# Even and odd last columns on two paths, target loaded further forward, and the rest column of target issued from ScalarE

## The chip, the cores and the metric

One core of one Trainium2 chip runs the kernel; the other seven are idle. The metric is device time in microseconds (us), the median of several executions. The profile's span (first to last instruction) is some 1.7 us shorter than that time. Executions of the kernel before agree within 0.05 us in six runs. All runs with rounds (repeated beside the kernel before) that are compared below are in the fast state, that is, none is over 1.5% above the fastest of its kernel; the one single look is marked.

## The reference

```python
# pred, target: (32, 147, 768) f32
mean = target.mean(-1, keepdims=True)
var = target.var(-1, keepdims=True)
target = (target - mean) / np.sqrt(var + 1e-6)
loss = np.mean((pred - target) ** 2, axis=-1)
return loss.mean(axis=-1)                      # (32,)
```

Both inputs are read once: 2 x 32 x 147 x 768 x 4 bytes = 28.9 MB. The output is 32 numbers.

## The kernel before

The 4704 rows lie on 128 partitions as 36 full "columns" of 128 rows and one "rest" column of 96 rows; a column is 128 x 768. VectorE takes mean and variance of each target column (two statistics, one aggregation), ScalarE and VectorE make `1/sqrt(var)`, GpSimd normalises into `s` (bf16). A *unit* is one or two columns, and its squared difference goes one of three ways:

- **"ACT"**: TensorE forms `pred - s` in PSUM (the memory that its products go to) with two identity products, ScalarE squares and sums it.
- **"DVE+ACT"**: VectorE subtracts in SBUF (the working memory), ScalarE squares and sums.
- **"DVE"**: VectorE subtracts, squares and sums.

Small matmuls with a mask add everything up at the end.

```python
# order of loads; "hw" = Sync's queue, f32; the others GpSimd's queue, f32 read, bf16 written
piece("t", 0, 4, q="hw"); piece("t", REST, REST + 1, q="hw")
# ... t4, p_rest, t8, p0, t12, t16, p4, t20, p8 ...
piece("t", 24, 28); piece("p", 12, 16)
piece("t", 28, 32); piece("p", 16, 20)
piece("t", 32, 36)
# ... pred 20 to 31 in twos, 32, 33, 34 alone, 35 in halves

groups = [tuple(range(0, 4)), (REST,)] + [tuple(range(c, c + 4)) for c in range(4, KM, 4)]
units = [((c, c + 1), 0, D, "ACT" if c < 22 else "DVE+ACT") for c in range(0, KM - 4, 2)]
# ... 28 "DVE", 29 "DVE+ACT", (30, 31) "DVE+ACT", 32 "DVE", 33 "DVE+ACT", 34 "DVE",
#     35 as two halves "ACT"

def normalise(u, c):                     # GpSimd
    # ...
    pin(nc.gpsimd.tensor_scalar(out=s[:n, so:so + D], in0=til[:n, o:o + D], scalar1=nm, scalar2=r,
                                op0=ALU.add, op1=ALU.mult))

def difference(u, d0, w):                # VectorE, two inputs in SBUF
    # ...
    pin(nc.vector.tensor_tensor(out=z[:, :w], in0=til[:, o:o + w], in1=s[:, so + d0:so + d0 + w],
                                op=ALU.subtract))

psum = ctx.enter_context(tc.tile_pool(name="psum", bufs=2, space=bass.MemoryType.PSUM))   # z: 3 banks each
```

Every operation is listed with an estimated duration, and a greedy list schedule in the kernel's own Python fixes each engine's program order. The engines then run in that order.

Of the kernel before, what the change touches and what calls it, by code (L numbers as in the profile page):

```python
# [7 lines left out]
F32 = mybir.dt.float32  # L8
BF16 = mybir.dt.bfloat16
ALU = mybir.AluOpType  # L10
ACTF = mybir.ActivationFunctionType
# [3 lines left out]
def kernel(  # L15
# [7 lines left out]
    nc = tc.nc  # L23
    pin = tc.keep_in_program_order
    B, N, D = pred.shape
    eps = 1e-6
    P = 128
    J = P // B
    KJ = (N + J - 1) // J
    KM = N - (J - 1) * KJ  # L30
    assert KJ == KM + 1
    RP = B * (J - 1)
    half = D // 2
    BANK = 512
    REST = KM
# [4 lines left out]
    def rows_of(c):  # L40
        return RP if c == REST else P

    data = ctx.enter_context(tc.tile_pool(name="data", bufs=1))
# [3 lines left out]
    singles = ctx.enter_context(tc.tile_pool(name="singles", bufs=1))  # L47
# [5 lines left out]
    stream = []  # L53

    def piece(kind, c0, c1, d0=0, d1=D, q="sw"):
        stream.append((kind, c0, c1, d0, d1, q))

    piece("t", 0, 4, q="hw")
    piece("t", REST, REST + 1, q="hw")
    piece("t", 4, 8)  # L60
    piece("p", REST, REST + 1)
    piece("t", 8, 12)
# [2 lines left out]
    piece("t", 16, 20)  # L65
    piece("p", 4, 8)
    piece("t", 20, 24)
    piece("p", 8, 12)
    piece("t", 24, 28)
    piece("p", 12, 16)  # L70
    piece("t", 28, 32)
    piece("p", 16, 20)
    piece("t", 32, 36)
    for c in range(20, 24, 2):
        piece("p", c, c + 2)
    for c in range(24, 32, 2):
        piece("p", c, c + 2)
    for c in range(32, 35):
        piece("p", c, c + 1)
# [1 line left out]
    piece("p", KM - 1, KM, half, D)  # L81


    groups = [tuple(range(0, 4)), (REST,)] + [tuple(range(c, c + 4)) for c in range(4, KM, 4)]


    units = [((c, c + 1), 0, D, "ACT" if c < 22 else "DVE+ACT") for c in range(0, KM - 4, 2)]
    units.insert(2, ((REST,), 0, D, "ACT"))
    units += [((KM - 4,), 0, D, "DVE"), ((KM - 3,), 0, D, "DVE+ACT"), ((KM - 2,), 0, D, "DVE"),
              ((KM - 1,), 0, half, "ACT"), ((KM - 1,), half, D, "ACT")]  # L90
    k = units.index(((KM - 8, KM - 7), 0, D, "DVE+ACT"))
    units[k:k + 1] = [((KM - 8,), 0, D, "DVE"), ((KM - 7,), 0, D, "DVE+ACT")]



# [3 lines left out]
    def op(name, engine, dur, needs, fn, rank=0.0, early=0.0):  # L99
        by_name[name] = len(ops)  # L100
        ops.append((name, engine, dur, needs, fn, rank, early))
# [4 lines left out]
    def load(kind, c0, c1, d0, d1, q):  # L106
        x = targ_f if kind == "t" else pred_f
        n, w = rows_of(c0), d1 - d0
        til = data.tile([P, (c1 - c0) * w], F32 if q == "hw" else BF16, name=f"{kind}{c0}_{d0}")
        src = bass.AP(tensor=x.tensor, offset=x.offset + c0 * D + d0,  # L110
                      ap=[[N * D, B], [KJ * D, J - 1 if c0 == REST else J], [1, (c1 - c0) * w]])
        eng = nc.sync if q == "hw" else nc.gpsimd
        pin(eng.dma_start(out=til[:n], in_=src))  # L113
        for c in range(c0, c1):
            KIND[kind].setdefault(c, []).append((d0, d1, til, (c - c0) * w))


    land, lanes, clock, last = {}, {"hw": [], "sw": []}, 2.9, {}
    for i, (kind, c0, c1, d0, d1, q) in enumerate(stream):
        w = (c1 - c0) * (d1 - d0)  # L120
        clock += w * rows_of(c0) / P * 0.915 / D + (0.0 if w >= 4 * D else 0.04)
        lanes[q].append(clock + 1.1)
        for c in range(c0, c1):
            land[kind, c, d0] = clock + 1.1
        k = len(lanes[q])
        op(("load", i), "SP" if q == "hw" else "POOL", 0.6, [], lambda a=stream[i]: load(*a), rank=-1.0,
           early=0.0 if k <= 8 else lanes[q][k - 9] + 0.3)

    def landed(kind, c):
# [124 lines left out]
        pin(nc.vector.scalar_tensor_tensor(out=z, in0=z, scalar=1.0, in1=z, op0=ALU.mult, op1=ALU.mult,  # L254
                                           accum_out=dest))

    tail = 4
    n_early = len(units) - 1 - tail
    rl = singles.tile([P, n_early], F32)
    rl_sum = singles.tile([P, 1], F32)  # L260
    finals = []
    early_ops, users, seen = [], [], set()
    for k, (u, d0, d1, eng) in enumerate(units):
        w = len(u) * D if len(u) > 1 else d1 - d0
# [32 lines left out]
        users.append(("sq", k))  # L297

    acc = psum1.tile([1, B], F32)
    op("rl_sum", "DVE", 0.2, early_ops, lambda: pin(nc.vector.tensor_reduce(  # L300
        out=rl_sum, in_=rl, axis=mybir.AxisListType.X, op=ALU.add)), rank=50.0)
    finals.insert(0, ("rl_sum", rl_sum, mask, P))
    turn = []

# [7 lines left out]

    HOP = 0.15
    free = {e: 0.0 for e in ("SP", "POOL", "DVE", "ACT", "PE")}
    free["ACT"] = 2.1
    end, left, order = {}, list(range(len(ops))), []
    while left:
        best = None
        for i in left:
            name, engine, dur, needs, fn, rank, early = ops[i]  # L320
            if any(x not in end for x in needs):
                continue
            t = max([free[engine], early] + [end[x] + (0.0 if ops[by_name[x]][1] == engine else HOP) for x in needs])
# [4 lines left out]
        _, i, t = best  # L328
        name, engine, dur, needs, fn, rank, early = ops[i]
# [43 lines left out]
```

## Time and profile before

| | before |
|---|---|
| time, us | 77.8 |
| span, us | 76.0 |
| HBM read over the span | 28.90 MB, 380 GB/s |
| VectorE, GpSimd, ScalarE busy | 69%, 71%, 41% |
| DMA traffic ends | about 71.0 |
| last normalisation on GpSimd ends | 69.2 |
| copy of the result starts | 73.85 |

The lines that carry the reading stand in the prediction below. Lines from the timeline of the end: start, duration, engine, what, count, in brackets the idle time before it and what ended it.

```profile
66.22 1.41 DVE L249 TENSOR_TENSOR zd<-p,s 128x768 bf16<-128x768 bf16 x2 [1.11 <-DMA p<-in_pred_dram]
68.44 2.50 DVE L249 TENSOR_TENSOR zd<-p,s 128x1536 bf16<-128x1536 bf16 x3
```

Two single columns in 1.41 us, then a pair and two singles in 2.50. The fastest single difference in this trace takes 0.54. GpSimd is normalising beside them until 69.2. The views merge neighbouring instructions; their single records in the trace show that only two of these differences are slow: column 28 takes 0.95 us, and the pair 30 and 31 takes 1.56, where a pair takes 0.92 to 0.96 elsewhere.

### The profile page before, as it was taken

The numbers are of one execution on the slowest core, as the hardware profiler recorded it, in microseconds if no ns is written. First come the engines' busy times: TensorE is split into PE (matmuls) and PEld (weight loads), VectorE is DVE, ScalarE is ACT, GpSimd is POOL, SyncE is SP. The second block draws the span as 40 slices with busy tenths as digits, with TensorE's granted clock in tenths as the row PEclk, the third lists the DMA queues.
The fourth block names the chain that finished last, engine by engine and source line by source line (L and its number), as shares of the span: only waits on it lengthen the run. The fifth ranks groups of instructions, "written<-read, shape, count | busy, mean of one in ns | idle before, by whom it ended". The sixth has DMA issues, their size and how long they took to land.

```text
span 76.0 us, 535 instructions
## 1 busy us (share of the span) xinstructions
PE 29.5 (39%) x85; PEld 8.8 (12%) x86; DVE 52.3 (69%) x139; ACT 31.1 (41%) x61; POOL 54.0 (71%) x76
## 2 busy tenths in 40 slices
PE   0000000056898940679187708751642200004550
PEld 0000000011323300212031103110111000001020
DVE  0000499999999999927960896099429995499960
ACT  5100000400269501088019503940591669952960
POOL 4998205299998987598986898984488839994000
PEclk9999999999999999999965995699999555555555
DMA  0899999999999999999999999999999999999400
GB/s 0 213 420 310 251 228 236 210 220 213 210 217 217 213 214 217 217 210 213 217 217 217 213 215 217 210 220 210 220 199 212 210 215 210 216 200 201 61 0 0
DMA packets 3830, 15.41 MB, mean 203 GB/s; under 512 B 435, under 2 KB 1171, under 8 KB 3699
## 3 DMA queue, kind: packets, MB, share of 16 engines
q0 software_dynamic: 3568, 13.52, 88.2%
q1 hardware_dynamic: 258, 1.87, 6.8%
q14 instruction: 4, 0.02, 0.1%
HBM read 28.90 MB, written 0.00 MB: 380 GB/s over the span
## 4 chain that ended last, share of the span: by engine, by line
DMA 66%; DVE 21%; POOL 7%; issue 2%; PE 1%; ACT 0%; POOLq 0%; DVEq 0%; ACTq 0%
DMA t<-in_target_dram 49%; DMA p<-in_pred_dram 17%; DVE st L163 13%; POOL s L213 6%; DVE mv L164 3%; DVE zd L254 3%; DVE zd L249 2%; POOL p L113 1%; PE acc L307 1%; ACT r L187 0%; DVE r L193 0%; DVE ob L336 0%; POOLq L213 0%; DVEq L249 0%; ACTq L187 0%
## 5 line engine op out<-in xcount | busy, mean ns | idle before, releaser
L163 DVE BATCH_NORM_STATS2 st<-t 128x6 f32<-128x384 bf16 (+2 forms) x74 | 36.1, 530 | 14.2 <-DMA t<-in_target_dram 14.2
L213 POOL TENSOR_SCALAR s<-t,nm,r 128x768 bf16<-128x768 bf16 (+2 forms) x37 | 38.2, 1038 | 4.3 <-DVE r L193 2.2
L227 PE MATMUL z<-s,nident 128*128 128x512 bf16 (+3 forms) x36 | 13.8, 499 | 31.3 <-POOL s L213 26.9
L242 ACT ACTIVATE z<-z 128x1536 f32<-128x1536 f32 (+2 forms) x13 | 17.0, 1311 | 12.0 <-PE z L227 12.0
L227 PE MATMUL z<-p,ident 128*128 128x512 bf16 (+3 forms) x35 | 14.2, 548 | 12.2 <-DMA p<-in_pred_dram 12.0
L113 POOL DMA_DIRECT2D p<-in_pred_dram x17 | 9.6, 566 | 9.2 <-DMA t<-in_target_dram 4.3
L187 ACT ACTIVATE r<-mv,eps_t 128x4 f32<-128x4 f32 (+1 forms) x10 | 2.9, 293 | 26.8 <-DVE mv L164 26.1
L249 DVE TENSOR_TENSOR zd<-p,s 128x768 bf16<-128x768 bf16 (+1 forms) x9 | 7.3, 842 | 2.1 <-DMA p<-in_pred_dram 1.1
L242 ACT ACTIVATE zd<-zd 128x1536 bf16<-128x1536 bf16 (+1 forms) x6 | 7.6, 1264 | 2.8 <-DVE zd L249 2.8
L164 DVE BATCH_NORM_AGGREGATE mv<-st 128x2 f32<-128x12 f32 (+1 forms) x37 | 7.7, 209 | 1.3
L227 PEld LDWEIGHTS <-nident 128*128 128x128 bf16 (+1 forms) x37 | 3.4, 113 | 42.3 <-issue 23.0
L227 PEld LDWEIGHTS <-ident 128*128 128x128 bf16 (+1 forms) x37 | 4.8, 129 | 19.8 <-issue 18.5
L113 POOL DMA_DIRECT2D t<-in_target_dram x8 | 4.8, 622 | 1.0 <-POOLq L354 0.8
L193 DVE RECIPROCAL r<-r 128x4 f32<-128x4 f32 (+1 forms) x10 | 1.5, 148 | 2.8 <-ACT r L187 2.8
L254 DVE SCALAR_TENSOR_TENSOR zd<-zd 128x768 bf16<-128x768 bf16 x3 | 2.8, 949 | 0.0
L242 ACT ACTIVATION_READ_ACCUMULATOR z<-z 128x1 f32 (+1 forms) x13 | 2.4, 188 | 0.0
L188 ACT ACTIVATE nm<-mv 128x4 f32<-128x4 f32 (+1 forms) x10 | 1.9, 189 | 0.0
L187 ACT ACT_TABLE_LOAD x1 | 1.3, 1283 | 0.8 <-PEq L354 0.8
L307 PE MATMUL acc<-mask,rl 128*1 128x32 f32 x8 | 1.0, 229 | 0.7 <-ACT zd L242 0.4
L242 ACT ACTIVATION_READ_ACCUMULATOR zd<-zd 128x1 f32 x6 | 1.1, 186 | 0.0
L152 DVE MEMSET eps_t<- 128x1 f32 x1 | 0.1, 59 | 0.9 <-PEq L354 0.9
L307 PEld LDWEIGHTS acc<-mask,rl 128*1 128x1 f32 x8 | 0.4, 87 | 1.9 <-ACT zd L242 1.3
(25 smaller groups left out, 5.7 us busy)
## 6 DMA issues: line engine op xcount, KB each, us to landing
t<-in_target_dram POOLq DMA_DIRECT2D x8, 768.0 KB, 26.1
p<-in_pred_dram POOLq DMA_DIRECT2D x5, 768.0 KB, 26.4
p<-in_pred_dram POOLq DMA_DIRECT2D x6, 384.0 KB, 22.3
t<-in_target_dram SPq DMA_DIRECT2D x1, 1536.0 KB, 7.9
p<-in_pred_dram POOLq DMA_DIRECT2D x3, 192.0 KB, 12.8
t<-in_target_dram SPq DMA_DIRECT2D x1, 288.0 KB, 10.6
p<-in_pred_dram POOLq DMA_DIRECT2D x2, 96.0 KB, 9.8
p<-in_pred_dram POOLq DMA_DIRECT2D x1, 144.0 KB, 10.5
```

What stands on the lines that cost most here:

```text
L113: pin(eng.dma_start(out=til[:n], in_=src))
L163: pin(nc.vector.bn_stats(out=st[:n, j, :], in_=x))
L164: pin(nc.vector.bn_aggr(out=out, in_=st[:n, :len(parts)]))
L187: pin(nc.scalar.activation(out=r[:n], in_=mv[:n, :, 1], func=ACTF.Sqrt, bias=eps_t[:n], scale=1.0))
L188: pin(nc.scalar.activation(out=nm[:n], in_=mv[:n, :, 0], func=ACTF.Copy, scale=-1.0))
L193: pin(nc.vector.reciprocal(out=rs[g][:n], in_=rs[g][:n]))
L213: pin(nc.gpsimd.tensor_scalar(out=s[:n, so:so + D], in0=til[:n, o:o + D], scalar1=nm, scalar2=r, op0=ALU.add, op1=ALU.mult))
L227: pin(nc.tensor.matmul(z[:n, a:b], eye[:n, :n], src[:n, so + a:so + b], start=first, stop=not first))
L242: pin(nc.scalar.activation(out=z[:n, :w], in_=z[:n, :w], func=ACTF.Square, accum_out=dest[:n]))
L249: pin(nc.vector.tensor_tensor(out=z[:, :w], in0=til[:, o:o + w], in1=s[:, so + d0:so + d0 + w], op=ALU.subtract))
L254: pin(nc.vector.scalar_tensor_tensor(out=z, in0=z, scalar=1.0, in1=z, op0=ALU.mult, op1=ALU.mult, accum_out=dest))
L307: pin(nc.tensor.matmul(acc, vec[:n], m[:n], start=len(turn) == 1, stop=len(turn) == len(finals)))
```

## The change

Its intent is that the last columns alternate between VectorE (even) and TensorE with ScalarE (odd), so that neither engine waits for the other; that target is in earlier, so that statistics and normalisations are over sooner; and that the rest column doesn't queue behind the first target load. The core of the diff (the schedule's bookkeeping for the third queue is left out):

```diff
-    piece("t", REST, REST + 1, q="hw")
+    piece("t", REST, REST + 1, q="hw2")          # ScalarE's queue
     ...
     piece("t", 20, 24)
+    piece("t", 24, 28)
     piece("p", 8, 12)
-    piece("t", 24, 28)
+    piece("t", 28, 32)
     piece("p", 12, 16)
-    piece("t", 28, 32)
-    piece("p", 16, 20)
     piece("t", 32, 36)
-    for c in range(20, 24, 2):
-        piece("p", c, c + 2)
-    for c in range(24, 32, 2):
+    for c in range(16, 32, 2):
         piece("p", c, c + 2)
     ...
+    groups = [tuple(range(0, 4)), (REST,)] + [tuple(range(c, c + 4)) for c in range(4, 16, 4)]
+    groups += [(c, c + 1) for c in range(16, KM, 2)]
+    units = [((c, c + 1), 0, D, "ACT" if c < 18 else "DVE+ACT") for c in range(0, 24, 2)]
+    units.insert(2, ((REST,), 0, D, "ACT"))
+    units += [((24,), 0, D, "DVE"), ((25,), 0, D, "DVE+ACT"), ((26, 27), 0, D, "DVE+ACT")]
+    units += [((c,), 0, D, "ACT" if c % 2 else "DVE") for c in range(28, KM - 1)]
+    units += [((KM - 1,), 0, half, "ACT"), ((KM - 1,), half, D, "ACT")]
     ...
-    tail = 4
+    tail = 5
     ...
-    op("rl_sum", "DVE", 0.2, early_ops, ... nc.vector.tensor_reduce(out=rl_sum, in_=rl, ...))
+    op("rl_sum", "ACT", 0.4, early_ops, ... nc.scalar.activation(out=junk, in_=rl, func=ACTF.Copy, accum_out=rl_sum))
```

More of the change, by code (lines that the diff above doesn't have):

```diff
@@ L81 @@
     piece("p", KM - 1, KM, half, D)
-    groups = [tuple(range(0, 4)), (REST,)] + [tuple(range(c, c + 4)) for c in range(4, KM, 4)]
-    units = [((c, c + 1), 0, D, "ACT" if c < 22 else "DVE+ACT") for c in range(0, KM - 4, 2)]
+    groups = [tuple(range(0, 4)), (REST,)] + [tuple(range(c, c + 4)) for c in range(4, 16, 4)]
+    groups += [(c, c + 1) for c in range(16, KM, 2)]
+    units = [((c, c + 1), 0, D, "ACT" if c < 18 else "DVE+ACT") for c in range(0, 24, 2)]
     units.insert(2, ((REST,), 0, D, "ACT"))
-    units += [((KM - 4,), 0, D, "DVE"), ((KM - 3,), 0, D, "DVE+ACT"), ((KM - 2,), 0, D, "DVE"),
-              ((KM - 1,), 0, half, "ACT"), ((KM - 1,), half, D, "ACT")]
-    k = units.index(((KM - 8, KM - 7), 0, D, "DVE+ACT"))
-    units[k:k + 1] = [((KM - 8,), 0, D, "DVE"), ((KM - 7,), 0, D, "DVE+ACT")]
+    units += [((24,), 0, D, "DVE"), ((25,), 0, D, "DVE+ACT"), ((26, 27), 0, D, "DVE+ACT")]
+    units += [((c,), 0, D, "ACT" if c % 2 else "DVE") for c in range(28, KM - 1)]
+    units += [((KM - 1,), 0, half, "ACT"), ((KM - 1,), half, D, "ACT")]
     ops, by_name = [], {}
@@ L108, in load @@
         n, w = rows_of(c0), d1 - d0
-        til = data.tile([P, (c1 - c0) * w], F32 if q == "hw" else BF16, name=f"{kind}{c0}_{d0}")
+        til = data.tile([P, (c1 - c0) * w], BF16 if q == "sw" else F32, name=f"{kind}{c0}_{d0}")
         src = bass.AP(tensor=x.tensor, offset=x.offset + c0 * D + d0,
                       ap=[[N * D, B], [KJ * D, J - 1 if c0 == REST else J], [1, (c1 - c0) * w]])
-        eng = nc.sync if q == "hw" else nc.gpsimd
+        eng = {"hw": nc.sync, "hw2": nc.scalar, "sw": nc.gpsimd}[q]
         pin(eng.dma_start(out=til[:n], in_=src))
@@ L115, in load @@
             KIND[kind].setdefault(c, []).append((d0, d1, til, (c - c0) * w))
-    land, lanes, clock, last = {}, {"hw": [], "sw": []}, 2.9, {}
+    land, lanes, clock = {}, {"hw": [], "hw2": [], "sw": []}, 2.9
     for i, (kind, c0, c1, d0, d1, q) in enumerate(stream):
@@ L125 @@
         k = len(lanes[q])
-        op(("load", i), "SP" if q == "hw" else "POOL", 0.6, [], lambda a=stream[i]: load(*a), rank=-1.0,
+        op(("load", i), {"hw": "SP", "hw2": "ACT", "sw": "POOL"}[q], 0.6, [], lambda a=stream[i]: load(*a), rank=-1.0,
            early=0.0 if k <= 8 else lanes[q][k - 9] + 0.3)
@@ L299, with early_sum @@
     acc = psum1.tile([1, B], F32)
-    op("rl_sum", "DVE", 0.2, early_ops, lambda: pin(nc.vector.tensor_reduce(
-        out=rl_sum, in_=rl, axis=mybir.AxisListType.X, op=ALU.add)), rank=50.0)
+    def early_sum():
+        junk = singles.tile([P, n_early], F32, name="junk")
+        pin(nc.scalar.activation(out=junk, in_=rl, func=ACTF.Copy, accum_out=rl_sum))
+    op("rl_sum", "ACT", 0.4, early_ops, early_sum, rank=50.0)
     finals.insert(0, ("rl_sum", rl_sum, mask, P))
@@ L314 @@
     free = {e: 0.0 for e in ("SP", "POOL", "DVE", "ACT", "PE")}
-    free["ACT"] = 2.1
+    free["ACT"] = 0.0
     end, left, order = {}, list(range(len(ops))), []
```

## The prediction

> **What bounds the kernel now.** I began with the page: its slices, its DMA part, its groups. No engine is full: VectorE is busy 69% of the span, GpSimd 71%. The DMA row is.
>
> ```profile
> DMA  0899999999999999999999999999999999999400
> GB/s 0 213 420 310 251 228 236 210 220 213 210 217 217 213 214 217 217 210 213 217 217 217 213 215 217 210 220 210 220 199 212 210 215 210 216 200 201 61 0 0
> HBM read 28.90 MB, written 0.00 MB: 380 GB/s over the span
> ```
>
> A slice is 1.9 us. From the third slice to the thirty-seventh the 16 DMA engines are at 9 tenths or more. The loads on GpSimd's queue read f32 and write bf16, so 215 GB/s written is 430 GB/s read; 28.9 MB at 430 is 67.2 us. Add some 2 us before the first bytes and the data cannot be in before about 69 to 71 us of a 76.0 us span. The change moves no byte, so only the two ends can give time: some 2 us before and 5 us after the data.
>
> Next I read the end: first the stretches (start:end and length; busy us with counts for PE, PE weight load, VectorE, ScalarE, GpSimd; clock; DMA share; GB/s).
>
> ```profile
> 70.50:71.00 0.50, 0.00 (x0) 0.00 (x0) 0.50 (x2) 0.50 (x1) 0.00 (x0) 0.50 1.00 149
> 71.00:71.50 0.50, 0.38 (x1) 0.10 (x1) 0.50 (x1) 0.50 (x2) 0.00 (x0) 0.50 0.08 11
> 71.50:72.00 0.50, 0.48 (x2) 0.00 (x0) 0.50 (x3) 0.50 (x3) 0.00 (x0) 0.50 0.00 0
> ```
>
> DMA traffic stops just after 71.0 us. The last two pieces (96 KB, the halves of pred column 35) were issued at 60.59 and 62.44 us. Their issue-to-landing times have a median of 9.8, and the shortest of all pred issues is 9.1, so the two are 10.5 and 9.1: they land at 71.09 and about 71.54. Then the timeline of the end:
>
> ```profile
> 69.25 0.48 PE L227 MATMUL z<-s,nident 128*128 128x384 bf16 x1 [9.82 <-POOL s L213]
> 71.12 0.48 PE L227 MATMUL z<-p,ident 128*128 128x384 bf16 x1 [1.08 <-DMA p<-in_pred_dram]
> 71.51 0.83 ACT L242 ACTIVATE zd<-zd 128x768 bf16<-128x768 bf16 x1
> 71.62 0.48 PE L227 MATMUL z_last<-p,ident 128*128 128x384 bf16 x1
> 72.32 0.96 DVE L254 SCALAR_TENSOR_TENSOR zd<-zd 128x768 bf16<-128x768 bf16 x1
> 72.34 0.47 ACT L242 ACTIVATE z<-z 128x384 f32<-128x384 f32 x1
> 72.84 0.47 ACT L242 ACTIVATE z_last<-z_last 128x384 f32<-128x384 f32 x1
> 73.20 0.17 DVE L300 TENSOR_REDUCE rl_sum<-rl 128x1 f32<-128x18 f32 x1
> 73.85 0.18 DVE L336 COPY ob<-acc 1x32 f32<-1x32 f32 x1 [0.49 <-PE acc L307]
> ```
>
> The reader is to see that the last data is not what ends it. The first half's difference is ready at 71.12 + 0.48 = 71.60, but ScalarE squares it only at 72.34, because it is still squaring column 33 (71.51), which VectorE handed over late. VectorE has run without a gap since 66.22: differences and squares of 28 to 34, then the sum of the early columns until 73.37. Both engines finish at 73.4, and the last sums, the copy at 73.85 and the write follow. The chain of waits says the same: its last long piece is a pred transfer that lands at 69.62, then VectorE alone to 73.30.
>
> Why is VectorE late? The four last normalisations on GpSimd, in the same stretch:
>
> ```profile
> 63.01 6.18 POOL L213 TENSOR_SCALAR s<-t,nm,r 128x768 bf16<-128x768 bf16 x4
> ```
>
> They take 1.55 us each against 0.98 undisturbed (the tile's view gives 0.98 to 2.45), and the single-column differences beside them average 0.63 against 0.55 alone. They run so late because target 32 to 35 lands at 56.6 us and its statistics end at 61.2.
>
> **What the Trainium skill says.** (1) "Trainium Kernel Development and Optimization", Key Constraints: transfers started from the Sync, Scalar and GpSimd queues run on the same 16 engines and interleave; several issuers save only issue time. Here one issue from the Sync queue costs some 0.6 us and the DMA row is full, so a second issuer should add no bandwidth; no run yet shows it. (2) "DMA: Bandwidth & Descriptors", Queues, rings and completion order: each engine goes round-robin among the queue rows that have work. The trace fits: the first target load (1.5 MB) lands at 8.71, although 1.5 MB alone would need only 3.7 us at 420 GB/s. (3) "GPSIMD Engine Reference", Specifications: GpSimd's memory interface is shared with VectorE and contended by VectorE instructions with two such inputs. The 1.55 against 0.98 agrees.
>
> **The change, part by part.**
> Rest column from ScalarE's queue. SP's second issue, at about 1.5 us, goes; ScalarE issues at about 0.8 instead, before its table load (1.28 us), whose result is first used at 13.4. Both are hidden. In 2.5 to 4.0 us the DMA share is only 0.51, 0.71 and 0.94: 0.5 x (0.49 + 0.29 + 0.06) = 0.4 us of engine time unused. An earlier third queue may fill a part; I take 0.1 us. Against it, a third row takes turns with the first target load: 0.29 MB at 420 GB/s is up to 0.7 us of delay for it, so statistics may start at about 9.3, not 8.73. VectorE waits 1.74 us for a target at 34.64, so this is absorbed.
>
> Target further forward. Target 24, 28 and 32 each go ahead of one 768 KB pred load, 4 columns x 0.915 = 3.7 us. Target 32 then lands at about 53, its statistics end at about 57.5, and the last normalisations end near 61 instead of 69.2. GpSimd has the room: from 14.7 us it owes 37 x 0.98 + 18 issues x 0.55 = 46 us, so it can't end before 61; I allow 63 with contention. Its norms then leave the last 7 us, and VectorE's differences return to 0.55.
>
> Smaller groups. 15 instead of 10: five more roots (0.29 + 0.19 on ScalarE) and reciprocals (0.15 on VectorE), 2.4 and 0.75 us, all before 58 and beside the transfers.
>
> Last columns on two paths. VectorE differences: 14 columns instead of 13 (+0.55); VectorE squares: five instead of three (+2 x 1.02). With the reciprocals and less the sum (0.17), VectorE gets 3.2 us more in all, from 52.3 to 55.5, in the 64 us from 8.7: it fits. What counts is the end. Landings of pred, from the waits and the 0.915 us per column: 28-29 at 66.2, 30-31 about 68.0, 32 at 68.6, 33 at 69.6, 34 at 70.5, halves at 71.1 and 71.5. VectorE does even columns, 0.55 + 0.95 + 0.08 = 1.6 each: 28 at 66.2 to 67.8, 30 at 68.0 to 69.6, 32 to 71.1, 34 to 72.7. ScalarE does odd ones through TensorE (0.79 + 0.19): 29 and 31 by 69.6, the sum of the early ones (about 0.4) in the gap, 33 from 70.3 to 71.3. It is then free when the first half is ready at 71.60: 71.62 to 72.21, second half 72.21 to 72.80. The kernel before takes 0.42 from ScalarE's last accumulator (73.43) to the copy (73.85), so the copy comes at 73.22 on ScalarE's path; VectorE's end at 72.7 is inside it.
> Sum: 73.85 - 73.22 = 0.63, plus 0.1 at the start: 0.7 us. 77.78 - 0.7 = 77.1.
>
> **Rivals.**
> (a) The DMA hides everything: nothing but the tail can go, 0.6 us or less. This is my main reading, with the DMA row for it.
> (b) VectorE or GpSimd becomes the bound. For: VectorE gets 3.2 us more, and four columns at 1.6 us against arrivals 0.95 apart leave it only 0.1 us ahead of ScalarE; one late normalisation gives the gain back, 77.6 to 77.9. Against: the gaps of 0.4 to 2.1 us in which it waits for target.
> (c) An in-order wait: ScalarE's sum of the early columns needs VectorE's square of 30; where it stands ahead of a ready square it holds it by up to 0.5 us: 77.5. Or GpSimd holds a pred issue behind a normalisation: each issue precedes its landing by 9 us or more, so this needs a long hold; I give it little.
> (d) The transfers end earlier. From 67 to 71 us they wrote 149 to 215 GB/s (mean about 195), while GpSimd and VectorE fought for memory. If that fight is the cause and it goes, 4 us x 9% = 0.35 us more: 76.7. More likely it is the small pieces, which stay.
>
> **Range and chances.** The terms known best, the landing of the last half and the 1.7 us behind it, are untouched, so the spread is small: (b) and (c) reach up to 77.8, (d) and a better start down to 76.6. Over 2% would need 76.2, that is 0.9 us off the transfers beyond the tail: 6%. Slower than 79.3 would need a new stall of 2 us: 2%.
>
> **What would show it.** Right: DMA share falls to zero within 0.3 us of 71.0; the first half is squared within 0.15 us of its matmul; no normalisation after 64; the copy at 73.0 to 73.4; the span near 75.3. Rest on its queue: the first target load lands later than 8.71 and nothing at the end moves. Wrong: DMA ends over 0.4 us away from 71.0 (then the start or the late rate was mis-sized), a gap on ScalarE before the early sum while a difference is ready, or VectorE ending after ScalarE.

## The result, and the profile after

| | before | after |
|---|---|---|
| median of 6 runs, us | 77.8 (77.77 to 77.82) | 77.13 (77.05 to 77.39) |
| span of the profiled run, us | 76.0 | 75.4 |
| VectorE busy, us | 52.3 | 56.3 |
| first target load landed | 8.71 | 9.23 |
| last normalisation ends | 69.2 | 65.2 |
| copy starts | 73.85 | 73.26 |

The ratio is 0.9922, 95% interval 0.9906 to 0.9938. It is formed from the single runs, so it is not quite the ratio of the two medians. It is a gain clear of noise, but less than 2%.

The page after, the two rows that answer to those of before, in slices of 1.9 us:

```profile
DMA  0899999999999999999999999999999999999700
GB/s 0 215 424 339 262 192 236 218 209 215 212 215 215 212 216 225 212 209 215 215 212 215 219 212 225 209 212 202 214 215 209 215 210 210 214 205 205 117 0 0
```

The transfers fill the same stretch. The stretches at the end (start:end, length, busy us of PE, PE weight load, VectorE, ScalarE, GpSimd, then clock, DMA share and GB/s):

```profile
70.50:71.00 0.50, 0.29 (x3) 0.19 (x3) 0.50 (x3) 0.37 (x1) 0.00 (x0) 0.50 0.94 140
71.00:71.50 0.50, 0.45 (x3) 0.05 (x2) 0.47 (x2) 0.50 (x2) 0.00 (x0) 0.50 0.06 8
```

Traffic ends just after 71.0, as before. So the 0.6 us came out of what follows the data. The timeline of the end:

```profile
70.63 0.80 ACT L239 ACTIVATE z<-z 128x768 f32<-128x768 f32 x1 [0.86 <-PE z L224]
71.05 0.48 PE L224 MATMUL z<-p,ident 128*128 128x384 bf16 x1 [0.26 <-DMA p<-in_pred_dram]
71.30 0.96 DVE L251 SCALAR_TENSOR_TENSOR zd<-zd 128x768 bf16<-128x768 bf16 x1
71.45 0.40 PE L307 MATMUL acc<-mask,rl 128*1 128x32 f32 x4
71.56 0.47 ACT L239 ACTIVATE z<-z 128x384 f32<-128x384 f32 x1
71.78 0.50 PE L224 MATMUL z_last<-p,ident 128*128 128x384 bf16 x1
72.32 0.47 ACT L239 ACTIVATE z_last<-z_last 128x384 f32<-128x384 f32 x1 [0.18 <-PE z_last L224]
73.26 0.18 DVE L336 COPY ob<-acc 1x32 f32<-1x32 f32 x1 [0.99 <-PE acc L307]
```

The reader is to see ScalarE at 71.56, 0.03 us behind the end of the first half's matmul; before, it came 0.74 us behind (71.60 to 72.34). The end now hangs on the last landing, through TensorE and ScalarE. There is one new flaw: two small final sums (71.45) stand in TensorE's order ahead of the last half, which starts only at 71.78.

GpSimd left the tail later than I had said, and not without a fight. The same timeline a little earlier:

```profile
57.45 2.69 DVE L246 TENSOR_TENSOR zd<-p,s 128x1536 bf16<-128x1536 bf16 x1
60.42 2.29 POOL L210 TENSOR_SCALAR s<-t,nm,r 128x768 bf16<-128x768 bf16 x1 [0.59 <-DVE r L190]
63.27 1.95 POOL L210 TENSOR_SCALAR s<-t,nm,r 128x768 bf16<-128x768 bf16 x1
65.18 0.56 POOL L110 DMA_DIRECT2D p<-in_pred_dram  x1
```

A pair's difference that takes 0.96 us alone took 2.69, a normalisation that takes 0.98 took 2.29 and 1.95, and the last pred issue came at 65.18 instead of 62.44. It still landed at about 71.5: the two half-column issues have a median of 7.3 us to landing, the first took 62.66 to 71.00 = 8.3, so the other took 6.3.

### The profile page after: what moved, and what is told of

It reads as the page before. It is cut to its first block, busy times and chain, and to the rows that moved or that the text cites. A ratio compares the mean times of both kernels' runs of the same rounds, so it can differ in the third digit from the quotient of the medians.

```text
span 75.4 us, 570 instructions
## 1 busy us (share of the span) xinstructions
PE 30.3 (40%) x87; PEld 8.7 (11%) x88; DVE 56.3 (75%) x148; ACT 32.0 (42%) x73; POOL 54.4 (72%) x77
## 3 DMA queue, kind: packets, MB, share of 16 engines
q1 hardware_dynamic: 146, 1.57, 5.7%
## 4 chain that ended last, share of the span: by engine, by line
DMA 60%; DVE 18%; POOL 9%; issue 6%; PE 2%; ACT 1%; POOLq 0%; ACTq 0%
DMA t<-in_target_dram 49%; DVE st L160 14%; DMA p<-in_pred_dram 11%; POOL s L210 8%; DVE mv L161 3%; DVE zd L246 1%; PE acc L307 1%; POOL t L110 1%; PE z L224 1%; ACT z_last L239 1%; PE z_last L224 1%; POOLq L368 0%; DVE r L190 0%; POOL p L110 0%; DVE ob L336 0%
## 5 line engine op out<-in xcount | busy, mean ns | idle before, releaser
L224 PE MATMUL z<-s,nident 128*128 128x512 bf16 (+4 forms) x36 | 14.6, 511 | 23.3 <-POOL s L210 17.6
L239 ACT ACTIVATE z<-z 128x1536 f32<-128x1536 f32 (+3 forms) x14 | 16.6, 1184 | 6.9 <-PE z L224 6.8
L224 PE MATMUL z<-p,ident 128*128 128x512 bf16 (+4 forms) x35 | 14.2, 542 | 12.1 <-DMA p<-in_pred_dram 12.0
L184 ACT ACTIVATE r<-mv,eps_t 128x2 f32<-128x2 f32 (+2 forms) x15 | 4.4, 293 | 29.5 <-DVE mv L161 28.8
L110 POOL DMA_DIRECT2D p<-in_pred_dram x18 | 10.2, 565 | 2.7 <-DVE st L160 1.0
L246 DVE TENSOR_TENSOR zd<-p,s 128x768 bf16<-128x768 bf16 (+1 forms) x10 | 9.7, 991 | 0.5 <-ACT zd L239 0.3
L239 ACT ACTIVATE zd<-zd 128x1536 bf16<-128x1536 bf16 (+1 forms) x5 | 6.7, 1345 | 2.7 <-DVE zd L246 2.7
L251 DVE SCALAR_TENSOR_TENSOR zd<-zd 128x768 bf16<-128x768 bf16 x5 | 4.8, 955 | 0.1
L190 DVE RECIPROCAL r<-r 128x2 f32<-128x2 f32 (+2 forms) x15 | 1.9, 123 | 1.7 <-ACT r L184 1.7
L185 ACT ACTIVATE nm<-mv 128x2 f32<-128x2 f32 (+2 forms) x15 | 2.8, 188 | 0.0
```

Source lines behind the costliest of these rows:

```text
L110: pin(eng.dma_start(out=til[:n], in_=src))
L184: pin(nc.scalar.activation(out=r[:n], in_=mv[:n, :, 1], func=ACTF.Sqrt, bias=eps_t[:n], scale=1.0))
L185: pin(nc.scalar.activation(out=nm[:n], in_=mv[:n, :, 0], func=ACTF.Copy, scale=-1.0))
L190: pin(nc.vector.reciprocal(out=rs[g][:n], in_=rs[g][:n]))
L224: pin(nc.tensor.matmul(z[:n, a:b], eye[:n, :n], src[:n, so + a:so + b], start=first, stop=not first))
L239: pin(nc.scalar.activation(out=z[:n, :w], in_=z[:n, :w], func=ACTF.Square, accum_out=dest[:n]))
```

## The experiments

The three parts can be had one by one. Eleven kernels ran, ten of them with 5 rounds beside the kernel before on the same chip (its medians there: 77.72 to 77.74).

| kernel | median, us | ratio to before | 95% interval |
|---|---|---|---|
| the full change | 77.13 | 0.9922 | 0.9906 to 0.9938 |
| rest column's queue alone | 77.73 | 0.9997 | 0.9984 to 1.001 |
| order of loads alone | 77.18 | 0.9924 | 0.9911 to 0.9936 |
| split of the last columns alone | 78.59 | 1.0114 | 1.0098 to 1.0129 |
| all but the rest column's queue | 77.25 | 0.9937 | 0.9925 to 0.995 |
| all but the split | 77.14 | 0.9923 | 0.991 to 0.9937 |
| all, early sum on VectorE | 77.31 | 0.9945 | 0.9932 to 0.9957 |
| order alone, four normalisations more | 79.21 | 1.0197 | 1.0183 to 1.0211 |
| before, four normalisations less | 77.18 | 0.9931 | 0.9916 to 0.9945 |
| last columns in halves | 77.3 | 0.9944 | 0.9931 to 0.9956 |
| all, TensorE's last order mended | 76.98 | 0.9898 | 0.9883 to 0.9914 |
| all, last pred in one piece (one look) | 78.79 | | |

My theory at the start was the prediction's: two engines queue behind each other in the tail, and the split frees them while the order only helps. The rivals were that the order is the whole cause, and that the third queue shortens the transfers.

### The rest column's queue alone

```diff
 # the kernel before
-    piece("t", REST, REST + 1, q="hw")
+    piece("t", REST, REST + 1, q="hw2")
```

> The kernel before with the rest column of target loaded from ScalarE's queue, nothing else. Theory (the gain is all in the tail, the transfers end where they did): 77.8 us, within 0.1 of the kernel before, with the first target load landing at about 9.2 instead of 8.7. Rival (an earlier third queue fills the half-idle DMA engines at 2.5 to 4 us and the transfers end earlier): 77.6 or less, with DMA traffic ending 0.2 us earlier.

No change: 0.9997. VectorE's timeline shows the side effect:

```profile
9.45 1.02 DVE L163 BATCH_NORM_STATS2 st<-t 128x6 f32<-128x384 f32 x2 [8.51 <-DMA t<-in_target_dram]
```

The first statistics start 0.7 us later than before (8.73). In the trace the rest column's packets now run from 5.2 us on, beside those of the first target load (2.2 to 8.5); before, they began only at 7.9, when that load's had ended. Nothing at the end moves. The queue gives no bandwidth.

### The order of loads alone

```diff
 # the kernel before
+    piece("t", 24, 28)
     piece("p", 8, 12)
-    piece("t", 24, 28)
+    piece("t", 28, 32)
     piece("p", 12, 16)
     ...                        # the load order of the change; groups, units, queues as before
```

> The kernel before with only the new order of loads (target 24, 28, 32 one pred load further forward). Theory (two engines queue up behind each other in the tail; the order only clears GpSimd out of it): about 77.5, since VectorE's last columns get faster by about 0.1 us each but ScalarE still squares column 33 before the last halves. Rival (late normalisations are the whole cause): 77.1, as the full change. Second rival (the order alone does nothing): 77.8.

77.18, the whole gain, where I had expected 77.5. My theory of the split fell here. Its timeline of the end:

```profile
66.08 1.03 DVE L246 TENSOR_TENSOR zd<-p,s 128x768 bf16<-128x768 bf16 x2 [0.72 <-DMA p<-in_pred_dram]
68.08 1.43 DVE L246 TENSOR_TENSOR zd<-p,s 128x1536 bf16<-128x1536 bf16 x2
69.88 0.56 DVE L246 TENSOR_TENSOR zd<-p,s 128x768 bf16<-128x768 bf16 x1 [0.38 <-DMA p<-in_pred_dram]
70.55 0.82 ACT L239 ACTIVATE zd<-zd 128x768 bf16<-128x768 bf16 x1
71.75 0.47 ACT L239 ACTIVATE z<-z 128x384 f32<-128x384 f32 x1 [0.28 <-PE z L224]
73.36 0.18 DVE L333 COPY ob<-acc 1x32 f32<-1x32 f32 x1 [0.49 <-PE acc L304]
```

Two single differences take 1.03 us instead of 1.41; VectorE even waits for the data of column 33 (0.38). So ScalarE squares column 33 at 70.55, not 71.51, and is idle when the first half comes. The old units are good enough once VectorE is undisturbed. GpSimd's last normalisation ended at 66.2 here.

### The split of the last columns alone

```diff
 # the kernel before: units, tail = 5 and the early sum on ScalarE as in the change; load order, groups, queues as before
```

> The kernel before with only the last columns split even to VectorE, odd to TensorE and ScalarE, and the early sum on ScalarE; loads and groups as before. Theory: it takes part of the gain, about 77.4, because normalisations at 63 to 69 us still slow VectorE and TensorE now waits for them too. Rival (the split is the whole cause): 77.1. Rival (without earlier target the split is worthless): 77.8 or more.

78.59: the split without the order loses 0.85 us. I had expected a gain. The timeline:

```profile
63.11 6.68 POOL L212 TENSOR_SCALAR s<-t,nm,r 128x768 bf16<-128x768 bf16 x4
69.84 0.48 PE L226 MATMUL z_last<-s,nident 128*128 128x384 bf16 x1 [3.03 <-POOL s L212]
70.99 0.80 ACT L241 ACTIVATE z<-z 128x768 f32<-128x768 f32 x1 [2.63 <-PE z L226]
74.79 0.18 DVE L338 COPY ob<-acc 1x32 f32<-1x32 f32 x1 [0.62 <-PE acc L309]
```

TensorE runs its products in program order, and the last half's product with the normalised column 35 stands ahead of column 31's difference. It waits 3.03 us for GpSimd, and ScalarE 2.63 for TensorE. On this path more work hangs on the late normalisations than before.

### All but the rest column's queue, and all but the split

```diff
 # the full change
-    piece("t", REST, REST + 1, q="hw2")
+    piece("t", REST, REST + 1, q="hw")
```

> The full change without the rest column's move: it stays on the Sync queue. Theory: 77.1 as the full change, within 0.1, first target load landing at 8.7. Rival (the queue gave part): 77.3 or more.

```diff
 # the full change; units, tail = 4 and the early sum on VectorE as before
```

> The full change without the new split of the last columns (units, tail and early sum as before; order, groups of two and rest queue as in the change). After the first four runs my theory is: the order is the whole gain, because it takes the late normalisations off the path to the last columns. It expects 77.15, ratio 0.991 to 0.994, as the order alone (0.9924). My first theory (the split is what gives the gain) expects 77.5 or more.

77.25 is 0.15 above 77.1, a little more than the 0.1 that I had allowed, and under the rival's 77.3. Its interval overlaps the full change's, so a gain of some 0.1 us from the queue is neither shown nor excluded. Its first statistics start at 8.63 again. And 77.14 without the split, ratio 0.9923 against 0.9922: the split and the move of the sum add nothing that can be measured on top of the order. In the trace the copy starts at 73.28 without the split and at 73.26 with it. The groups of two and the rest column's queue, which this kernel has and the order alone has not, don't show either (0.9923 and 0.9924).

### Is it GpSimd's company that costs the time?

The order does two things at once: it ends VectorE's statistics earlier, and it takes GpSimd's normalisations out of the last microseconds. Two kernels tell these apart. The first puts the normalisations back without anything waiting for them:

```diff
 # the order of loads alone
+    for c in range(32, 36):            # after the last normalisation, into spare tiles
+        pin(nc.gpsimd.tensor_scalar(out=spare, in0=til[:, o:o + D], scalar1=nm, scalar2=r,
+                                    op0=ALU.add, op1=ALU.mult))
```

> The kernel before with the new order of loads, and four more normalisations on GpSimd after the last one, into spare tiles that nobody reads: GpSimd is busy again to about 70 us, but nothing waits for it. Contention theory (GpSimd's work beside VectorE's differences is what cost the time): VectorE's last single-column differences go back from 0.55 to over 0.7 us and the time to 77.5 or more. Lateness theory (the last columns waited for the normalisations' results, not for the memory): 77.2, as the order alone.

79.21, 2 us more than the order alone, though nobody reads the spare tiles. The timeline:

```profile
65.96 7.87 POOL L302 TENSOR_SCALAR spare<-t,nm,r 128x768 bf16<-128x768 bf16 x4
66.92 1.57 DVE L251 SCALAR_TENSOR_TENSOR zd<-zd 128x768 bf16<-128x768 bf16 x1
68.59 2.50 DVE L246 TENSOR_TENSOR zd<-p,s 128x1536 bf16<-128x1536 bf16 x3
```

Each of VectorE's three squares takes 1.54 to 1.57 us instead of 0.96, and the three differences 2.50 as before; GpSimd's four take 1.97 each instead of 0.98. In one point the expectation missed: no single difference went over 0.7 (they took 0.54 to 0.59); the pair, with 1.56 instead of 0.96, and the squares took the loss. The size is not that of the kernel before either: the spare normalisations run to 73.8 us, beside VectorE's last square, where the old ones ended at 69.2. So this run shows that such company costs time, not how much it cost before. The second takes the normalisations away from the kernel before, its loads in the old order:

```diff
 # the kernel before; wrong result on purpose
-        s, so = sbuf[u[0]]
+        s, so = sbuf[u[0] - 4 if 32 <= u[0] < REST else u[0]]      # columns 32 to 35 use s of 28 to 31
     ...                                                            # their four normalisations are left out
```

> The kernel before, loads in their old order, without the normalisations of columns 32 to 35: these columns take the normalised target of 28 to 31 instead (a wrong result on purpose; everything else stays). GpSimd is then empty from about 64 us. Contention theory: VectorE's single differences fall from 0.63 to 0.55 on average and its squares stay at 0.95, ScalarE meets the last halves in time, 77.2 as with the new order. Rival (what the new order gave is the earlier end of the statistics on VectorE, not GpSimd's absence): 77.7, as before.

77.18: the whole gain, without touching the order, the groups or VectorE's statistics, which still end at about 61. In its timeline the first half is squared at 71.70 and the copy starts at 73.27:

```profile
66.38 1.03 DVE L249 TENSOR_TENSOR zd<-p,s 128x768 bf16<-128x768 bf16 x2 [1.25 <-DMA p<-in_pred_dram]
71.70 0.47 ACT L242 ACTIVATE z<-z 128x384 f32<-128x384 f32 x1
73.27 0.18 DVE L336 COPY ob<-acc 1x32 f32<-1x32 f32 x1 [0.49 <-PE acc L307]
```

That settles it: the time before was lost to GpSimd working beside VectorE between 63.0 and 69.2 us, and the order gives it back by ending that earlier. Two rivals are ruled out by the traces. VectorE does the last columns in the same sequence in all three kernels (before, order alone, this one), so no changed program order is at work. And in the kernel before nothing at the end waited for a late result: the normalisation of column 34 ended at 66.76 and its difference began at 71.73; that of column 35 ended at 69.20, and its pred came only at 71.1. Column 28 takes 0.56 us here instead of 0.95, the pair 30 and 31 takes 0.95 instead of 1.56: these two are the 1.0 us that VectorE lost before. Part of it VectorE now spends waiting for data (0.17 us for column 33 here, 0.38 with the order alone).

The single records also show how the time is lost. It is not a general slowing down. Over all thirteen traces 22 of VectorE's differences and squares after 55 us took more than 1.2 us, and 20 of them ended 0.80 to 0.82 us after a normalisation on GpSimd had ended: the pair of the kernel before at 70.00, behind 69.20; the three squares with spare normalisations at 68.50, 72.58 and 74.64, behind 67.69, 71.77 and 73.83. They end as if they had stood until GpSimd was done. The other two ended 1.4 us after one, with a DMA issue of GpSimd in between.

### The early sum back on VectorE

> The full change with the early sum back on VectorE. Theory: the sum lies in a gap on either engine, so 77.1 within 0.15. Rival (the sum at VectorE's end was on the path to the copy): 77.3 or more.

77.31, just outside what I had allowed and where the rival stood. Its interval (0.9932 to 0.9957) overlaps that of the full change (0.9906 to 0.9938) by a little. In its trace the copy starts at 73.34, 0.08 us later. I call it unclear: the medians differ by 0.2 us, and it is open whether the sum is the cause.

### Two attempts at a better end

```diff
 # the full change
+  ((32,), 0, D, "ACT"), ((33,), 0, half, "DVE"), ((33,), half, D, "ACT"),
+  ((34,), 0, half, "DVE"), ((34,), half, D, "ACT"), ((35,), 0, half, "ACT"), ((35,), half, D, "DVE")
```

> An attempt at a better end: the full change, with columns 33 and 34 cut in halves, one to each path, column 32 to ScalarE, the last half of column 35 to VectorE, the early sum on VectorE, and the late final sums on TensorE only after the last difference. Theory (after the last landing at 71.5 the time left is ScalarE doing two halves one after the other): both engines end near 72.4, copy at 72.8, time 76.7. Rival (more and smaller pieces of work cost as much as they save): 77.1.

A miss: 77.3. The timeline shows why:

```profile
71.12 0.48 PE L226 MATMUL z<-s,nident 128*128 128x384 bf16 x1 [0.41 <-ACT z L241]
72.02 0.47 ACT L241 ACTIVATE z<-z 128x384 f32<-128x384 f32 x1 [0.45 <-PE z L226]
```

A half takes a whole `z` buffer, and there are two. The product for column 34's half had to wait for ScalarE to leave one (0.41 us), then ScalarE waited for it (0.45).

```diff
 # the full change; TensorE's program order only
-        op(("final", i), "PE", 0.2, [need, "masks"], ...)
+        op(("final", i), "PE", 0.2, [need, "masks"] + ([("pred", len(units) - 1)] if i > 2 else []), ...)
+        # and the first half's difference needs final 2 (column 32), so that this one goes ahead
```

> The full change, with TensorE's order at the end mended: the small final sum of column 33, which stands ahead of the last half's difference and holds it from 71.53 to 71.78 us, goes behind it, and that of column 32 ahead of the first half's. Theory (every step behind the last landing counts one for one): z_last's difference starts at about 71.55, copy at 73.05, time 76.95. Rival (ScalarE's turn decides): 77.1.

76.98, the lowest time of all (0.9898). Against the full change's 0.9922 the intervals still touch, and the two never ran in the same rounds, so a gain of some 0.2 us is likely and not shown. The trace:

```profile
71.72 0.48 PE L224 MATMUL z_last<-p,ident 128*128 128x384 bf16 x1
72.25 0.48 ACT L239 ACTIVATE z_last<-z_last 128x384 f32<-128x384 f32 x1
73.20 0.18 DVE L336 COPY ob<-acc 1x32 f32<-1x32 f32 x1 [0.75 <-PE acc L307]
```

The last half no longer waits behind a final sum, but it starts at 71.72 and not at the 71.55 that I had expected, and the copy at 73.20 and not at 73.05. The data came later in this run: VectorE and TensorE start on columns 30 and 31 at 67.95 and 67.87, TensorE in the full change's trace at 67.68. That shift of 0.19 us is about what is missing. The final sums that now stand behind the last half don't delay the copy: from ScalarE's last accumulator it takes 0.36 us, as in the full change.

### What slows the last transfers

```diff
 # the full change
-    for c in range(32, 35):
-        piece("p", c, c + 1)
-    piece("p", KM - 1, KM, 0, half)
-    piece("p", KM - 1, KM, half, D)
+    piece("p", 32, 36)
```

> The full change with pred columns 32 to 35 in one piece of 768 KB instead of five small ones. The tail will be longer, since all four columns land at once: 79 or more. What is asked is when the DMA traffic ends. If small pieces cause the fall from 213 to 205 GB/s written after 66 us, it ends at about 70.7; if not, at 71.0 as in all the other runs.

78.79 us, a little under the 79 that I had expected. Its stretches and the first product after the landing:

```profile
66.00:69.00 3.00, 1.73 (x5) 0.65 (x5) 2.35 (x5) 2.06 (x5) 0.00 (x0) 0.50 1.10 223
69.00:70.50 1.50, 1.15 (x5) 0.28 (x4) 0.70 (x2) 1.11 (x4) 0.00 (x0) 0.50 0.99 205
70.50:71.00 0.50, 0.03 (x1) 0.06 (x1) 0.00 (x0) 0.00 (x0) 0.00 (x0) 0.50 0.16 25
71.73 1.12 PE L221 MATMUL z<-p,ident 128*128 128x512 bf16 x3 [1.20 <-DMA p<-in_pred_dram]
```

In 66 to 69 us it writes 223 GB/s, where the full change writes 205 in the same stretch, and by this view traffic is all but over at about 70.6 instead of 71.0. Here the view flatters the big piece, since it counts a whole packet at the packet's start. With each packet's bytes spread over its duration it is 214 against 209 GB/s in 66 to 69 us and 213 against 203 in 69 to 70.5. The packets' own records say why: one of the half columns takes 79 ns for 768 bytes, one of the single columns 135 ns for 1536, one of the big piece 474 ns for 6144, that is 59 ns for 768. So the small pieces do slow the transfers, by some 2 to 5% in this one look.

The big piece gained nothing by its rate. Its last packet ran from 70.91 to 71.39, when all its others had ended by 71.0; the full change's last packet ended at 71.20. Both landed some 0.3 us after their last packet, at 71.7 and 71.5.

## Why the prediction was right

The time (77.13 against 77.1), the copy (73.26 against 73.22) and the span (75.4 against 75.3) agree. So close an agreement is in part luck: runs of the changed kernel differ by 0.34 us, and some terms below cancel. Step by step:

- **Bound.** Right. DMA traffic ends at 71.0 in both kernels, and only what follows the data gave time.
- **Why VectorE is late.** Right, and shown twice: four normalisations more cost 2 us, four less in the old kernel give the whole gain. But the line was misread: 0.63 us is the mean of all five single columns, four of which took 0.54 to 0.55. The loss sat in one single column (0.95) and in the pair (1.56 instead of 0.95), which the prediction does not name.
- **Rest column's queue.** The mechanism was right (first target load at 9.23, delay absorbed). The 0.1 us at the start was not there: alone the queue gives 0.9997.
- **Target further forward.** Target 32 landed at 52.8 (predicted 53) and its statistics ended at 57.5 (57.5). The end of the normalisations, "I allow 63", was 65.2. The contention was sized too small: the pair's difference took 2.69 us (57.45 to 60.13) and held VectorE's last reciprocal until 60.06, so that the last two normalisations began only at 60.42, and these took 2.29 and 1.95 us themselves. "No normalisation after 64" is thereby wrong, without effect on the time. The sum before it counts 18 issues from 14.7 us on; by the trace 10 of the 26 on GpSimd's queue are over by then, so 16 are left and the earliest end is 60, not 61.
- **Smaller groups.** Hidden, as said.
- **Last columns on two paths.** VectorE's total was 56.3 us, not 55.5: its differences took 9.7, where 7.3 before and 0.55 more had been worked out. The sum came out, but the step was given to the wrong part. I worked out the end for the change as a whole and never for the order alone. With the order alone ScalarE also meets the first half at once (71.75, against 71.24 + 0.48 = 71.72 for the end of its matmul). The split by itself gains nothing, and without the order it loses 0.85 us. ScalarE was to be done with column 33 at 71.3, with 0.3 us to spare; it squared it from 70.63 to 71.53 and was just in time for the first half at 71.56. Within the sum two terms were off and in part cancelled: the second half's square started at 72.32 and not 72.21, because final sums stood before its matmul; from ScalarE's last accumulator to the copy it took 0.36 (72.90 to 73.26), not 0.42.
- **Rivals.** (b) did not come. (c) came in part: GpSimd held the last pred issue by 2.7 us, and it landed in time all the same. (d) is refuted: with GpSimd gone from 66 to 69 us the transfers wrote 205 GB/s, with GpSimd full 204 before. The small pieces are the likely cause, by their packets' times and by the one look of the last experiment.

## What to carry to other kernels

When an engine is slow in the tail, look at what its neighbours do at that moment, not only at its own list of work: moving three loads forward gave as much here as removing the neighbour's work, and redistributing the columns gave nothing. Where a change has several parts, work out the end for each part alone, not only for the sum. Splitting work over two engines lost 0.85 us here where its inputs came late, gained nothing that could be measured where they came early, and in halves it stalled on too few buffers. And look at the single records before averaging: a mean of 0.63 us hid the one slow column, and left out the slow pair beside it.

## What the Trainium skill lacked or had wrong

- "GPSIMD Engine Reference", Specifications, names the contention with VectorE's two-input instructions; that row gives no size. Other pages of the skill say more on how the two engines block each other, so this is a gap of the row and not of the skill. Here it is large and goes both ways: a difference of two columns took 2.69 us instead of 0.96, a square 1.57 instead of 0.96, a normalisation 2.29 instead of 0.98. The statistics, which read one tensor, took 0.96 to 1.0 us for two beside normalisations of 0.98, undisturbed.
- "DMA: Bandwidth & Descriptors", Bandwidth, says that for transfers between HBM and SBUF the HBM side (about 358 GB/s) binds. With one core running, these kernels wrote 215 GB/s of bf16 from f32, that is 430 GB/s read, through most of the span; the single-core measurement of 425 on the same page fits, the sentence does not as it stands. The same section gives 358 as each core's part when both cores of a memory pair stream, which no run here tests.
